# A row-sum kernel on one core: 120 consecutive rows per partition instead of 112, and 8 of the last 1,024 instead of 16

## The chip, the cores and the metric

The kernel runs on one core of a Trainium2 chip. Its time is the device time of one execution in microseconds (us); the median of several runs counts. Of the core's engines it uses VectorE (DVE in the profile), ScalarE (ACT) and SyncE (SP), which only issues transfers, and sixteen DMA engines that carry them.

## The reference

```python
batch, seq, dim = 32, 512, 1024
x = np.random.randn(batch, seq, dim).astype(np.float32)
multiplier = 0.5

def reference(x, multiplier):
    return (np.sum(x, axis=-1) * multiplier).astype(np.float32)
```

There are 32 x 512 = 16,384 rows of 1,024 numbers (4 KiB each, 64 MiB in all). Each row is summed and the sum halved; 64 KiB of results are written.

## The kernel before

The 16,384 rows are 128 per partition. They are cut in two regions. In the first, `x_rows` (line 43), each partition owns `own` = 112 consecutive rows; in the second, `x_last` (line 44), it owns 16 of the last 2,048. The results follow the same cut, `out_rows` and `out_last`, so that each partition's results are one run of bytes in each.

Rows are read in blocks of `B` = 16 per partition, 64 KiB per partition and 8 MiB in all, into three buffers `xb0` to `xb2`. All loads are issued by SP, so they share one DMA queue and stand in it in the order of issue. `load` (line 73) makes a load wait until the reduction that last read its buffer is done (`dve_done`), and gives each load a semaphore of its own. The first three loads wait for nothing; `start_loads_at_entry` puts them ahead of the kernel's start-up barrier.

Blocks 0 to 6 are the first region. For each, DVE waits for the load, sums the 16 rows in one `reduce_sum` (line 117) and multiplies the sums by 0.5 into `res` (line 123). In block 6 the last 8 rows go to ACT, one row per instruction (`act_row`, line 81, whose `accum_out` gives the scaled sum).

Block 7 is the second region. It is loaded in pieces of falling size, rows 0 to 7, 8 to 12, 13 to 14, and the last row in two parts of 544 and 480 numbers, so that little work is left when the last bytes land. Each piece's rows are split between ACT (`on_act`) and DVE (`dve_sum`, line 90, which adds the two halves of a row in one pass); the last row's two parts go to DVE.

There are two stores, both on SP. The early store (line 150) writes `res[:, 0:own]`; it waits for block 6 on DVE and on ACT and is issued once SP has issued all loads. The last store (line 175) writes `res[:, own:]` after the last row. SP then waits for both to land.

Of the kernel before, what the change touches and what calls it, by code (L numbers as in the profile page):

```python
# [9 lines left out]
def kernel(  # L10
# [13 lines left out]
    nc = tc.nc  # L24
# [10 lines left out]
    rows = N // P  # L35
    out_flat = out.rearrange("b s -> (b s)")
    mul = float(multiplier)

    B = 16
    n_blocks = rows // B  # L40
    assert N == P * rows and rows == n_blocks * B
    own = rows - B
    x_rows = x_flat[0 : P * own, :].rearrange("(p c) d -> p c d", p=P)
    x_last = x_flat[P * own : N, :].rearrange("(p c) d -> p c d", p=P)
    out_rows = out_flat[0 : P * own].rearrange("(p c) -> p c", p=P)
# [2 lines left out]
    def sbuf(name, *shape):  # L48
        return ctx.enter_context(nc.sbuf_tensor(name, list(shape), fp32)).ap()
# [4 lines left out]
    res = sbuf("res", P, rows)  # L54
    cut = 544
    at = 576
    end = sbuf("end", P, at + D - cut)

    def sem(name):
        return nc.alloc_semaphore(name=name)  # L60
# [5 lines left out]
    def marks(i, engine):  # L66

        s = dve_done if engine == "dve" else act_done
        i.then_inc(s, 1)
        counts[engine] += 1  # L70
        return counts[engine]

    def load(name, dst, src, free=None):
        landed = sem(name)
        i = nc.sync.dma_start(out=dst, in_=src)  # L75
        if free is not None:
            i.wait_op(dve_done, free, "sem-ge")
        i.then_inc(landed, 16)
        return landed

    def act_row(t, r, col):
        return nc.scalar.activation(  # L82
            out=t[:, r, :],
            in_=t[:, r, :],
            func=mybir.ActivationFunctionType.Copy,
            scale=mul,
            accum_out=res[:, col : col + 1],
        )

    def dve_sum(row, dst, scale):  # L90
        mid = row.shape[-1] // 2
        return nc.vector.tensor_tensor_reduce(  # L92
            out=row[:, 0:mid],
            in0=row[:, 0:mid],
            in1=row[:, mid:],
            scale=scale,
            scalar=0.0,
            op0=ADD,
            op1=ADD,
            accum_out=dst,  # L100
        )
# [3 lines left out]
    for b in range(n_blocks - 1):  # L105
        c0 = b * B
        t = buf[b % bufs]
        landed = load(
            f"landed{b}",
            t,  # L110
            x_rows[:, c0 : c0 + B, :],
            freed[b - bufs] if b >= bufs else None,
        )
        h = B if b < n_blocks - 2 else B // 2
        nc.vector.wait_ge(landed, 16)
        done = marks(
            nc.vector.reduce_sum(  # L117
                out=sums[:, c0 : c0 + h], in_=t[:, 0:h, :], axis=mybir.AxisListType.X
            ),
            "dve",  # L120
        )
        freed.append(done)
        scaled = nc.vector.tensor_single_scalar(  # L123
            out=res[:, c0 : c0 + h],
            in_=sums[:, c0 : c0 + h],
            scalar=mul,
            op=mybir.AluOpType.mult,
        )
        scaled.wait_op(dve_done, done, "sem-ge")
        early_dve = marks(scaled, "dve")  # L130
        if h < B:
            nc.scalar.wait_ge(landed, 16)
            for r in range(h, B):
                i = act_row(t, r, c0 + r)
            early_act = marks(i, "act")

    c0 = (n_blocks - 1) * B
    t = buf[(n_blocks - 1) % bufs]
    nc.sync.wait_ge(dve_done, freed[n_blocks - 1 - bufs])
    pieces = [(0, 8), (8, 13), (13, 15)]  # L140
    landed = [
        load(f"landed_p{k}", t[:, lo:hi, :], x_last[:, lo:hi, :])
        for k, (lo, hi) in enumerate(pieces)
    ]
    landed_end = [
        load(f"landed_e{k}", end[:, to : to + hi - lo], x_last[:, B - 1, lo:hi])
        for k, (to, lo, hi) in enumerate(((0, 0, cut), (at, cut, D)))
    ]
    nc.sync.wait_ge(dve_done, early_dve)
    early = nc.sync.dma_start(out=out_rows, in_=res[:, 0:own])  # L150
    early.wait_op(act_done, early_act, "sem-ge")
    early_stored = sem("early_stored")
    early.then_inc(early_stored, 16)

    on_act = {4, 5, 6, 7, 11, 12, 14}
    for k, (lo, hi) in enumerate(pieces):
        on = [r for r in range(lo, hi) if r in on_act]
        nc.scalar.wait_ge(landed[k], 16)
        for r in on:
            i = act_row(t, r, c0 + r)  # L160
        late_act = marks(i, "act") if k == len(pieces) - 1 else None
        on = [r for r in range(lo, hi) if r not in on_act]
        nc.vector.wait_ge(landed[k], 16)
        for r in on:
            dve_sum(t[:, r, :], res[:, c0 + r : c0 + r + 1], mul)
    nc.vector.wait_ge(landed_end[0], 16)
    first = dve_sum(end[:, 0:cut], end[:, at - 1 : at], 1.0)
    part = marks(first, "dve")
# [75 lines left out]
```

## Time and profile before

| What | Value |
|---|---|
| median of 3 runs | 160.72 us (160.71 to 160.73) |
| profiled execution | 160.73 us, span 159.4 us |
| DVE, ACT busy | 119.3 us (75%), 17.3 us (11%) |
| DMA packets, bytes | 2,016, 67.18 MB |
| early store | 56 KB, 10.8 us from issue to landing |
| last store | 8 KB, 1.4 us from issue to landing |

The profile is one execution; the span is the time between its first and last recorded event, and the time of the execution includes 1.3 us around it. In the timeline an instruction's row ends with the idle time of its engine before it and what ended it, in square brackets; "L117" is line 117 of the kernel. "SPq" is SP issuing a transfer, which is not the transfer itself. A packet is the part of a transfer that belongs to one partition here: 128 per load or store, eight for each DMA engine.

### The profile page before, as it was taken

The numbers are of one execution on the slowest core, as the hardware profiler recorded it, in microseconds if no ns is written. First come the engines' busy times: TensorE is split into PE (matmuls) and PEld (weight loads), VectorE is DVE, ScalarE is ACT, GpSimd is POOL, SyncE is SP. The second block draws the span as 40 slices with busy tenths as digits, with TensorE's granted clock in tenths as the row PEclk, the third lists the DMA queues.
The fourth block names the chain that finished last, engine by engine and source line by source line (L and its number), as shares of the span: only waits on it lengthen the run. The fifth ranks groups of instructions, "written<-read, shape, count | busy, mean of one in ns | idle before, by whom it ended". The sixth has DMA issues, their size and how long they took to land.

```text
span 159.4 us, 123 instructions
## 1 busy us (share of the span) xinstructions
DVE 119.3 (75%) x35; ACT 17.3 (11%) x31; POOL 0.2 (0%) x4
## 2 busy tenths in 40 slices
DVE  0000059998699968999599995999959999598644
ACT  3000000000000000000000000000000000397954
POOL 0000000000000000000000000000000000000000
DMA  7996996996998979969969969969979899698994
GB/s 263 526 526 263 526 526 263 526 510 280 526 428 362 526 345 444 526 280 510 526 263 526 526 263 526 510 280 526 477 312 526 378 411 526 288 493 359 437 402 143
DMA packets 2016, 67.18 MB, mean 421 GB/s; under 512 B 480, under 2 KB 608, under 8 KB 736
## 3 DMA queue, kind: packets, MB, share of 16 engines
q1 hardware_dynamic: 2016, 67.18, 98.0%
HBM read 67.11 MB, written 0.07 MB: 421 GB/s over the span
## 4 chain that ended last, share of the span: by engine, by line
DMA 76%; DVE 22%; SPq 1%; issue 0%
DMA xb<-in_x_dram 51%; DMA end<-in_x_dram 25%; DVE sums L117 22%; SPq L75 1%; DVE end L92 0%; DVE res L123 0%; DVE res L92 0%
## 5 line engine op out<-in xcount | busy, mean ns | idle before, releaser
L117 DVE TENSOR_REDUCE sums<-xb 128x16 f32<-128x16384 f32 (+1 forms) x7 | 112.0, 16001 | 30.8 <-DMA xb<-in_x_dram 30.8
L82 ACT ACTIVATE xb<-xb 128x1024 f32<-128x1024 f32 x15 | 15.7, 1045 | 137.7 <-DMA xb<-in_x_dram 137.7
L92 DVE CUSTOM_DVE_ANT_0 xb<-xb 128x512 f32<-128x512 f32 x8 | 5.1, 688 | 5.0 <-DMA xb<-in_x_dram 5.0
L82 ACT ACTIVATION_READ_ACCUMULATOR xb<-xb 128x1 f32 x15 | 2.8, 187 | 0.0
L103 DVE MEMSET end<- 128x2 f32 x1 | 0.1, 60 | 2.5 <-PEq L26 2.5
L82 ACT ACT_TABLE_LOAD x1 | 1.3, 1283 | 2.4 <-PEq L26 2.4
L123 DVE TENSOR_SCALAR res<-sums 128x16 f32<-128x16 f32 (+1 forms) x7 | 1.2, 174 | 0.2
L92 DVE CUSTOM_DVE_ANT_0 end<-end 128x272 f32<-128x272 f32 (+1 forms) x2 | 0.9, 426 | 0.2 <-DMA end<-in_x_dram 0.2
L92 DVE DVE_READ_ACCUMULATOR2_ANT res<- 128x1 f32 x9 | 0.7, 82 | 0.0
L225 POOL MEMSET const-bfloat16-1.0<- 128x1 bf16 x1 | 0.1, 101 | 0.0
L225 POOL MEMSET const-uint8-127<- 128x1 uint8 x1 | 0.1, 101 | 0.0
L225 POOL MEMSET const-float32-0.0<- 128x1 f32 x1 | 0.1, 98 | 0.2 <-issue 0.2
L225 POOL MEMSET const-float32-1.0<- 128x1 f32 x1 | 0.1, 98 | 0.0
L92 DVE DVE_READ_ACCUMULATOR2_ANT end<- 128x1 f32 x1 | 0.1, 83 | 0.0
## 6 DMA issues: line engine op xcount, KB each, us to landing
xb<-in_x_dram SPq DMA_DIRECT2D x1, 4096.0 KB, 31.1
xb<-in_x_dram SPq DMA_DIRECT2D x1, 2560.0 KB, 36.9
xb<-in_x_dram SPq DMA_DIRECT2D x1, 1024.0 KB, 38.9
end<-in_x_dram SPq DMA_DIRECT2D x1, 272.0 KB, 39.1
end<-in_x_dram SPq DMA_DIRECT2D x1, 240.0 KB, 39.2
xb<-in_x_dram SPq DMA_DIRECT2D x7, 40.8
out_dram<-res SPq DMA_DIRECT2D x1, 56.0 KB, 10.8
out_dram<-res SPq DMA_DIRECT2D x1, 8.0 KB, 1.4
```

Source lines behind the costliest of these rows:

```text
L75: i = nc.sync.dma_start(out=dst, in_=src)
L82: return nc.scalar.activation(out=t[:, r, :], in_=t[:, r, :], func=mybir.ActivationFunctionType.Copy, scale=mul, accum_out=res[:, col : co ...
L92: return nc.vector.tensor_tensor_reduce(out=row[:, 0:mid], in0=row[:, 0:mid], in1=row[:, mid:], scale=scale, scalar=0.0, op0=ADD, op1=ADD, ...
L103: marks(nc.vector.memset(end[:, at - 2 : at], 0.0), "dve")
L117: nc.vector.reduce_sum(out=sums[:, c0 : c0 + h], in_=t[:, 0:h, :], axis=mybir.AxisListType.X),
L123: scaled = nc.vector.tensor_single_scalar(out=res[:, c0 : c0 + h], in_=sums[:, c0 : c0 + h], scalar=mul, op=mybir.AluOpType.mult,)
L225: nc = _bacc.Bacc("TRN2", target_bir_lowering=False, num_devices=1)
```

## The change

`own` becomes 120: each partition owns 120 consecutive rows (480 KiB) in the first region and 8 of the last 1,024 (32 KiB) in the second. The loads keep their sizes and their order. The first piece of the last block (8 rows per partition) is now rows 112 to 119 of the first region; the pieces of 5 and 2 rows and the last row come from the second. The early store writes 120 results per partition (480 bytes, formerly 448) and waits for the first piece on DVE and ACT instead of for block 6; the last store writes 8 (32 bytes, formerly 64). The loop over the pieces therefore stands ahead of the early store in the text.

```diff
-    own = rows - B
+    tail = B // 2
+    own = rows - tail
 ...
-        early_dve = marks(scaled, "dve")
         if h < B:
             nc.scalar.wait_ge(landed, 16)
             for r in range(h, B):
-                i = act_row(t, r, c0 + r)
-            early_act = marks(i, "act")
+                act_row(t, r, c0 + r)
 ...
     pieces = [(0, 8), (8, 13), (13, 15)]
+    sources = [x_rows[:, c0:own, :], x_last[:, 0:5, :], x_last[:, 5:7, :]]
     landed = [
-        load(f"landed_p{k}", t[:, lo:hi, :], x_last[:, lo:hi, :])
-        for k, (lo, hi) in enumerate(pieces)
+        load(f"landed_p{k}", t[:, lo:hi, :], src)
+        for k, ((lo, hi), src) in enumerate(zip(pieces, sources))
     ]
     landed_end = [
-        load(f"landed_e{k}", end[:, to : to + hi - lo], x_last[:, B - 1, lo:hi])
+        load(f"landed_e{k}", end[:, to : to + hi - lo], x_last[:, tail - 1, lo:hi])
         for k, (to, lo, hi) in enumerate(((0, 0, cut), (at, cut, D)))
     ]
+
+    on_act = {4, 5, 6, 7, 11, 12, 14}
+    for k, (lo, hi) in enumerate(pieces):
+        nc.scalar.wait_ge(landed[k], 16)
+        nc.vector.wait_ge(landed[k], 16)
+        for r in range(lo, hi):
+            if r in on_act:
+                last_act = act_row(t, r, c0 + r)
+            else:
+                last_dve = dve_sum(t[:, r, :], res[:, c0 + r : c0 + r + 1], mul)
+        if k == 0:
+            early_act = marks(last_act, "act")
+            early_dve = marks(last_dve, "dve")
+    late_act = marks(last_act, "act")
     nc.sync.wait_ge(dve_done, early_dve)
     early = nc.sync.dma_start(out=out_rows, in_=res[:, 0:own])
     early.wait_op(act_done, early_act, "sem-ge")
 ...
-    on_act = {4, 5, 6, 7, 11, 12, 14}
-    for k, (lo, hi) in enumerate(pieces):
-        ...
```

More of the change, by code (lines that the diff above doesn't have):

```diff
@@ L153 @@
     early.then_inc(early_stored, 16)
-    on_act = {4, 5, 6, 7, 11, 12, 14}
-    for k, (lo, hi) in enumerate(pieces):
[L157 to L165, printed above, removed]
     nc.vector.wait_ge(landed_end[0], 16)
```

## The prediction

> **What bounds the kernel now.** I read the page first: its head, the engine shares, the slices and the DMA lines.
>
> ```profile
> span 159.4 us, 123 instructions
> ...
> DVE 119.3 (75%) x35; ACT 17.3 (11%) x31; POOL 0.2 (0%) x4
> ...
> DMA  7996996996998979969969969969979899698994
> ...
> q1 hardware_dynamic: 2016, 67.18, 98.0%
> HBM read 67.11 MB, written 0.07 MB: 421 GB/s over the span
> ...
> DMA 76%; DVE 22%; SPq 1%; issue 0%
> ```
>
> VectorE (DVE) is busy for 75% of the span, the DMA packets fill 98.0% of what sixteen DMA engines could do in it, and there is one queue, q1. So the transfers are the bound. The 22% that the chain gives to DVE says otherwise at first sight, so I read the chain of waits in order of time, and then the DVE rows of the timeline (start, duration, then what ended the idle time before).
>
> ```profile
> 0.43 40.72 DMA xb<-in_x_dram
> ...
> 118.30 39.18 DMA end<-in_x_dram
> 157.48 0.03 issue
> 157.51 0.41 DVE end L92
> ```
>
> ```profile
> 99.23 17.22 DVE L117 TENSOR_REDUCE sums<-xb 128x16 f32<-128x16384 f32 x1 [1.92 <-DMA xb<-in_x_dram]
> ...
> 118.57 17.22 DVE L117 TENSOR_REDUCE sums<-xb 128x16 f32<-128x16384 f32 x1 [1.91 <-DMA xb<-in_x_dram]
> ...
> 137.93 8.69 DVE L117 TENSOR_REDUCE sums<-xb 128x8 f32<-128x8192 f32 x1 [1.93 <-DMA xb<-in_x_dram]
> ...
> 146.91 0.35 SPq L150 DMA_DIRECT2D out_dram<-res  x1
> ...
> 147.64 0.69 DVE L92 CUSTOM_DVE_ANT_0 xb<-xb 128x512 f32<-128x512 f32 x1 [0.82 <-DMA xb<-in_x_dram]
> ...
> 151.72 0.19 ACT L82 ACTIVATION_READ_ACCUMULATOR xb<-xb 128x1 f32 x1
> 153.74 1.06 ACT L82 ACTIVATE xb<-xb 128x1024 f32<-128x1024 f32 x1 [1.84 <-DMA xb<-in_x_dram]
> ...
> 157.96 0.34 SPq L175 DMA_DIRECT2D out_dram<-res  x1
> ```
>
> Before every reduction DVE idles for about 1.9 us until a load lands, so each of these starts marks a landing: 118.57 - 99.23 = 19.34 and 137.93 - 118.57 = 19.36 us for 8 MiB, or 433 GB/s, with no hole between loads. A DVE link of 17.23 us in the chain only says which reduction freed a buffer; the load that it released then waited its turn (40.7 us to landing, two loads' worth). The span is therefore start (first reduction at 21.84, 2.5 us above one load of 19.35), then loads end to end until the last landing at 157.5, then a tail of 0.4 us on DVE and one small store (157.96 to 159.37, its 1.4 us to landing). The profiled execution took 160.73 us, 1.3 us around its span of 159.4; the median of the runs is 160.72, so the sum can be made against either.
>
> **The change, part by part.** The order of instructions on each engine is unchanged by the edit: DVE, ScalarE (ACT) and SP run the same instructions in the same order, seven loads of 64 KiB per partition, then 32, 20, 8, 2.1 and 1.9 KiB, then two stores. Four things differ.
>
> *1. The addresses of the loads.* Partitions now start 480 KiB apart in x instead of 448; the piece of 32 KiB per partition moves from the last region (64 KiB apart) to the main one (480); the pieces behind it are 32 KiB apart instead of 64. No row shows 480 or 32, so I bound by those that are there. At 448 KiB, 8 MiB take 19.36 us (433 GB/s). At 64 KiB, piece 0 takes 147.64 - 137.93 = 9.71 us for 4 MiB (432 GB/s), piece 1 153.74 - 147.64 = 6.10 us for 2.5 MiB (430). The trace's records of single packets, one per partition and load, explain the small fall by packet size alone: median 2,418 ns for 65,536 bytes, 1,213 for 32,768, 762 for 20,480, 311 for 8,192, 88 for 2,176, 25 for 448. All lie within 2 ns of 8 ns + bytes / 27.2 per ns. Eight packets per engine make the intervals: 8 x 2.418 = 19.34, 8 x 1.213 = 9.70, 8 x 0.762 = 6.10. A sevenfold change of the distance, odd multiple or power of two, thus left no mark on a packet. I take 0. The bounds: if the 56 large packets of an engine (56 x 2.418 = 135.4 us) ran at piece 1's rate instead of their own (433.4 / 429.7, 0.9%), the cost would be +1.2 us; in the other direction nothing below 8 ns + bytes / 27.2 is seen, except at the start, which is the second rival.
>
> A rule that speaks against such a change: the Trainium skill, "DMA: Bandwidth & Descriptors", section "Latency and other measured facts", lists copies between HBM tensors whose rows lie a large power of two apart as slow, 207 GB/s at 512 KiB and 103 at 4 MiB where 214 is full, and says that 4 KiB of padding restores it. By it 512 KiB would cost an estimated 3%, near 4.6 us here, while 480 KiB, which is 32 KiB off, would cost nothing; 32 KiB is a power of two, but below anything in its list. No run here shows 512 KiB.
>
> *2. The early store waits for more.* Before, SP waits for the last scaling by 0.5 (146.65 + 0.17) and issues 56 KB at 146.91. Now it waits for piece 0: DVE's fourth row ends near 150.2, ACT's row 7 at 151.72 + 0.19 = 151.91, so the issue moves to about 151.95, 5.0 us later. Behind it on SP there is only the wait for ACT's last row and the last store, which goes out at 157.96; all loads were issued by 118.8. On the ring the store stands behind the loads in either kernel: its packets first run at 156.5 and it lands at 146.91 + 10.8 = 157.7, just after the last load (157.48). From issue to first packet the last store needs 158.80 - 157.96 = 0.84 us, so the early one is ready near 152.8, 3.7 us ahead of its turn. Cost 0. Without that cover (issue after 155.7) it would slide later one for one, and would still have until 159.37 before it ended last.
>
> *3. The sizes of the stores.* Early: 480 bytes per partition instead of 448, by the line above 25.7 ns instead of 24.5; eight per engine, +0.01 us, ended long before 158.8. Last: 32 bytes instead of 64, 9.2 instead of 10.4 ns, 8 x 1.2 = -0.01 us on the path. What a 32-byte write costs in its confirmation no row shows. The time from the last packet's end to the last count of its semaphore is 0.38 us for the 64-byte store, 0.43 for the 1,920-byte load, 0.52 for the 448-byte store. So between -0.05 (a little less to confirm) and +0.14 (the dearest of those rows); I take the nearest row, the 64-byte one, hence 0.
>
> *4. The marks.* Two semaphore increments move from block 6's last instructions to piece 0's last; as many increments and waits as before, none on the path. 0.
>
> Sum: 160.73 + 0 + 0 - 0.01 + 0 = 160.72 against the profiled execution, 160.71 against the median. What is late stays late: the last load at 157.5.
>
> **The rivals.** *Slower: 480 KiB makes the DMA engines collide in the memory.* Place: the 56 large packets of each engine. Sixteen engines read in near lockstep (a load's sixteen completions lie within 0.5 us), each four partitions from its neighbour, formerly 1,792 and now 1,920 KiB. For it: the very first sixteen packets, which do start together, are the one group that is slow, 3.01 us in the mean against 2.42. Against it: all the later packets, at two distances, without a mark, and 1,920 = 15 x 128 is less even than 1,792 = 7 x 256. Price: at piece 1's rate +1.2 us, 161.9; if each of the seven loads lost the 0.59 us of the first wave, +4.1, 164.8. It decides from 0.32 us / 56 = 6 ns per packet, a median of 2,424. I take 161.9 as its time.
>
> *Faster: the first wave was a collision, and the new distance ends it.* The last engine to start (1.83 us) needed 2.74 us for its first packet, 0.32 above the rest, and the mean excess is 0.59; as the engines never idle afterwards, such a gain would reach the end: 160.1 to 160.4, say 160.3. Against it: the sixteen starts spread over 1.01 to 1.83, yet the first packets end between 4.02 and 4.57 almost regardless of their start (start 1.01 ends 4.29, start 1.52 ends 4.02), which looks like a common delay before the first data and not like addresses.
>
> *The stores decide.* A dear 32-byte confirmation, or one that comes early: +0.14 or -0.05 as above, which stays within 0.2%. To leave it, it would have to add another 0.2 us.
>
> **How the numbers follow.** 0.2% is 0.32 us, about what a measurement of this kernel can tell from no change. No change 0.68, at 160.6 to 160.9 (the bounds of the last store). Collisions 0.17. Faster first wave 0.09. The last store beyond its rows 0.06, 0.04 of it slower and 0.02 faster. So faster 0.09 + 0.02 = 0.11, same 0.68, slower 0.17 + 0.04 = 0.21. The range goes down to the faster rival's 160.3 and up to the slower one's 161.9, which leaves out about half of that rival and the lower part of the other, some 0.12.
>
> **What would show it.** Right: reductions still 19.35 us apart, large packets at 2,418 ns, early store issued near 152 with about 5.8 us to landing, last store 1.4 us. Collisions: intervals above 19.4 and a median above 2,424. The start: the first reduction before 21.5. The stores: a last landing other than 1.4 us after its issue. I am wrong if the time leaves 160.4 to 161.0 while the intervals between landings stay as they are.

## The result and the profile after

The changed kernel takes 160.94 us (median of 21 runs, 160.85 to 161.24), the kernel before 160.75 in the same comparison (21 runs, 160.62 to 161.12): a ratio of 1.0013, with a 95% interval of 1.0007 to 1.0018. It is slower by 0.2 us. The profiled executions say the same, 160.93 against 160.73.

The page of the changed kernel has the totals of before (the head, the engines, the queue, and the two stores with KB and us from issue to landing).

```profile
span 159.6 us, 123 instructions
...
DVE 119.3 (75%) x35; ACT 17.3 (11%) x31; POOL 0.2 (0%) x4
...
q1 hardware_dynamic: 2016, 67.18, 98.0%
...
out_dram<-res SPq DMA_DIRECT2D x1, 60.0 KB, 5.8
out_dram<-res SPq DMA_DIRECT2D x1, 4.0 KB, 1.4
```

The timeline of the changed kernel (start, duration, engine, line, operation, then the idle time before and what ended it), at the rows that the prediction used:

```profile
22.05 17.22 DVE L118 TENSOR_REDUCE sums<-xb 128x16 f32<-128x16384 f32 x1 [19.53 <-DMA xb<-in_x_dram]
41.38 17.22 DVE L118 TENSOR_REDUCE sums<-xb 128x16 f32<-128x16384 f32 x1 [1.90 <-DMA xb<-in_x_dram]
...
99.43 17.22 DVE L118 TENSOR_REDUCE sums<-xb 128x16 f32<-128x16384 f32 x1 [1.93 <-DMA xb<-in_x_dram]
...
118.78 17.22 DVE L118 TENSOR_REDUCE sums<-xb 128x16 f32<-128x16384 f32 x1 [1.92 <-DMA xb<-in_x_dram]
...
138.13 8.69 DVE L118 TENSOR_REDUCE sums<-xb 128x8 f32<-128x8192 f32 x1 [1.92 <-DMA xb<-in_x_dram]
...
147.84 0.69 DVE L93 CUSTOM_DVE_ANT_0 xb<-xb 128x512 f32<-128x512 f32 x1 [0.82 <-DMA xb<-in_x_dram]
...
152.13 0.35 SPq L164 DMA_DIRECT2D out_dram<-res  x1
...
158.16 0.34 SPq L178 DMA_DIRECT2D out_dram<-res  x1
```

And the first reduction of the kernel before, in its timeline:

```profile
21.84 17.22 DVE L117 TENSOR_REDUCE sums<-xb 128x16 f32<-128x16384 f32 x1 [19.31 <-DMA xb<-in_x_dram]
```

The last 139 us are the old ones, shifted: every row shown starts 0.20 or 0.21 us later (22.05 against 21.84, 138.13 against 137.93, 158.16 against 157.96), but for the early store, which has moved as foreseen. From the start of the first reduction to the end of the execution it is 160.93 - 22.05 = 138.88 us, and 160.73 - 21.84 = 138.89 before. All of the 0.2 us lie in front of the first reduction, in the landing of load 0.

The packet records show where. Each of the sixteen DMA engines carries eight packets of load 0, one after the other. (The records name no engine, but in both kernels every later packet of the seven large loads starts within 0.02 us of the end of an earlier one, so they fall into sixteen chains.) In the kernel before, the sixteen first packets take 3.02 us in the mean and the last of them ends 4.57 us into the span; now they take 3.23 us and the last ends at 4.78. The seven behind it take 2.42 us each in the mean in both kernels, so the first reduction starts 17.27 us after that last end in both (21.84 - 4.57, 22.05 - 4.78). Since no engine rests in these loads, whoever is late after its first packet is still late behind them.

### The profile page after: what moved, and what is told of

It reads as the page before. It is cut to its first block, busy times and chain, and to the rows that moved or that the text cites. A ratio compares the mean times of both kernels' runs of the same rounds, so it can differ in the third digit from the quotient of the medians.

```text
span 159.6 us, 123 instructions
## 1 busy us (share of the span) xinstructions
DVE 119.3 (75%) x35; ACT 17.3 (11%) x31; POOL 0.2 (0%) x4
## 4 chain that ended last, share of the span: by engine, by line
DMA 76%; DVE 22%; SPq 1%; issue 0%
DMA xb<-in_x_dram 51%; DMA end<-in_x_dram 25%; DVE sums L118 22%; SPq L76 1%; DVE end L93 0%; DVE res L93 0%
```

## Experiments

Theory 1: the places that load 0's first packets read set how far the last engine lags. Rivals: the stores; all loads at the new distance; a start that differs between any two programs. Each comparison has its own runs of the kernel before, whose medians lay between 160.73 and 160.82 us; the ratio follows the means of the runs, so that it can differ from the quotient of two medians where the runs scatter (452 KiB: 160.68 to 161.14). "Distance" is from the start of one partition's rows to the start of the next one's. The kernels that read rows of load 0, or of all loads, from elsewhere sum those other rows and serve only to measure time; "block 3 first" and the kernels with a head return the reference's results. "Last first packet" is the end, in us from the span's start, of the latest of the sixteen first packets of load 0, from the packet records; "rest" is the profiled execution less the start of its first reduction.

| Kernel | load 0's distance | last first packet | first reduction | rest | median | ratio (95%) |
|---|---|---|---|---|---|---|
| before | 448 KiB | 4.57 | 21.84 | 138.89 | 160.75 | 1 |
| changed | 480 | 4.78 | 22.05 | 138.88 | 160.94 | 1.0013 (1.0007 to 1.0018) |
| new stores, old reads | 448 | 4.60 | 21.89 | 138.89 | 160.79 | 1.0000 (0.9992 to 1.0009) |
| old, load 0 at 480 | 480 | 4.69 | 21.95 | 138.96 | 160.97 | 1.0013 (1.0004 to 1.0022) |
| new, load 0 at 448 | 448 | 4.59 | 21.86 | 138.92 | 160.78 | 1.0000 (0.9991 to 1.0009) |
| old, load 0 at 512 | 512 | 5.19 | 22.48 | 138.92 | 161.39 | 1.0039 (1.0027 to 1.0052) |
| old, load 0 at 64 | 64 | 4.67 | 21.92 | 138.94 | 160.86 | 1.0007 (0.9998 to 1.0016) |
| old, load 0 at 452 | 452 | 4.80 | 22.09 | 139.05 | 160.98 | 1.0006 (0.9997 to 1.0015) |
| old, load 0 at 416 | 416 | 5.33 | 22.60 | 138.93 | 161.46 | 1.0033 (1.0020 to 1.0046) |
| old, load 0 at 4 | 4 | 3.95 | 21.62 | 138.97 | 160.54 | 0.9984 (0.9975 to 0.9993) |
| old, block 3 first | 448 | 4.64 | 21.92 | 138.98 | 160.90 | 1.0009 (1.0000 to 1.0018) |
| new, block 3 first | 480 | 4.60 | 21.89 | 138.89 | 160.80 | 0.9999 (0.9991 to 1.0008) |
| old, all of x_rows at 512 | 512 | 5.08 | 22.38 | 139.09 | 161.47 | 1.0038 (1.0026 to 1.0050) |
| changed, once more | 480 | 4.67 | 21.97 | 138.92 | 160.97 | 1.0015 (1.0006 to 1.0024) |

**The change taken apart.** The first run puts all reads of the changed kernel back:

```diff
-    x_rows = x_flat[0 : P * own, :].rearrange("(p c) d -> p c d", p=P)
-    x_last = x_flat[P * own : N, :].rearrange("(p c) d -> p c d", p=P)
+    x_rows = x_flat[0 : P * (rows - B), :].rearrange("(p c) d -> p c d", p=P)
+    x_last = x_flat[P * (rows - B) : N, :].rearrange("(p c) d -> p c d", p=P)
...
-    sources = [x_rows[:, c0:own, :], x_last[:, 0:5, :], x_last[:, 5:7, :]]
+    sources = [x_last[:, lo:hi, :] for lo, hi in pieces]
...
-        load(f"landed_e{k}", end[:, to : to + hi - lo], x_last[:, tail - 1, lo:hi])
+        load(f"landed_e{k}", end[:, to : to + hi - lo], x_last[:, B - 1, lo:hi])
```

> The changed kernel with the addresses of all its loads put back to those before (448 KiB apart, the last block from the last 2,048 rows), so it stores sums of other rows in places; stores, their sizes and the early store's later issue stay as changed. Theory 1 (the 0.2 us come from the addresses of the first load, whose first sixteen packets end later): about 160.75 us, first reduction starts near 21.84. Rival (the stores, or the early store's later issue): about 160.94 and the first reduction near 21.84. Rival (something about the start that differs between any two programs): first reduction anywhere from 21.7 to 22.1, and the time with it.

The second and third exchange load 0 alone:

```diff
+    x_first = x_flat[0 : P * 120, :].rearrange("(p c) d -> p c d", p=P)   # P * 112 in the changed kernel
...
-            x_rows[:, c0 : c0 + B, :],
+            (x_first if b == 0 else x_rows)[:, c0 : c0 + B, :],
```

> The kernel before with one edit: block 0 is read with partitions 480 KiB apart instead of 448 (so block 0's sums are of other rows). Theory 1: about 160.94, first reduction near 22.05, all later reductions 19.35 apart. Rival (every load at 480 loses a little): about 160.77, 0.03 of the 0.2. Rival (stores): 160.75.

> The changed kernel with one edit: block 0 is read with partitions 448 KiB apart (its sums are of other rows); loads 1 to 7 and the stores stay as changed. Theory 1: about 160.75, first reduction near 21.84. Rivals (all loads, or the stores): about 160.92.

The first reduction in the timelines of these three, in this order:

```profile
21.89 17.22 DVE L118 TENSOR_REDUCE sums<-xb 128x16 f32<-128x16384 f32 x1 [19.38 <-DMA xb<-in_x_dram]
```

```profile
21.95 17.22 DVE L118 TENSOR_REDUCE sums<-xb 128x16 f32<-128x16384 f32 x1 [19.43 <-DMA xb<-in_x_dram]
```

```profile
21.86 17.22 DVE L119 TENSOR_REDUCE sums<-xb 128x16 f32<-128x16384 f32 x1 [19.34 <-DMA xb<-in_x_dram]
```

Load 0 at 480 KiB brings the whole 0.13% into the old kernel (160.97); load 0 at 448 takes all of it out of the changed one (160.78), whose other loads and stores stay changed; and the new stores with the old reads show no cost (1.0000). Theory 1 stands and the three rivals fall: no part of the stores or of loads 1 to 7 is seen, and the intervals leave them at most 0.09%. A start that differs between any two programs falls too: three programs with the old places of load 0 start at 21.84, 21.89 and 21.86 us, two with the new ones at 22.05 and 21.95. In the second run's profile the start moved by 0.11 instead of 0.21 us; one profile is one draw (the changed kernel once more gave 21.97), and the medians carry the size.

> The changed kernel once more, for the spread of its first wave: first reduction 21.95 to 22.1, 160.95 us, 0.13% above the kernel before. If it lies at 21.85 in this profile while the median stays at 160.95, one profile is not enough to rank two addresses.

It measured 160.97 us, 1.0015, so the effect repeats.

**Is there a rule in the distance?** The same edit with other values of rows per partition in `x_first`: 128, 16, 113 and 104, and, as the last, a pattern that lets partition p start at row p.

> The kernel before with block 0 read with partitions 512 KiB apart (other rows). Theory 1 in the form that engines collide when their addresses differ by a large power of two: the first packets last longer than the 3.0 and 3.2 us means seen, the first reduction starts after 22.05, by 0.2 to some us. Theory 1 without that form (any address has its own start): between 21.7 and 22.2. No effect of addresses: 21.84 and 160.75.

> The kernel before with block 0 read with partitions 64 KiB apart, one run of 8 MiB (other rows). Theory A (the first packets of the sixteen engines collide when the addresses four partitions apart, here 256 KiB, share a large power of two; 448 gives 7 x 256 KiB): a start as with 448, first reduction 21.85 to 21.9, 160.8 us. Theory B (the first touch of far-apart places costs; 64 KiB keeps the whole load in 8 MiB instead of some 56): a start better than with 448, first reduction 21.2 to 21.6, 160.2 to 160.5.

> The kernel before with block 0 read with partitions 452 KiB apart (113 rows; four partitions are 113 x 16 KiB apart). Theory A: fewer collisions than any distance before, first reduction 21.3 to 21.7, 160.2 to 160.6 us. Theory B: as with 448, 21.85 and 160.8.

> The kernel before with block 0 read with partitions 416 KiB apart (104 rows; four partitions are 13 x 128 KiB apart, as 480 gives 15 x 128). Theory A: as with 480, first reduction 21.95 to 22.05, 161.0 us. Theory B: as with 448, 21.85 and 160.8.

> The kernel before with block 0 read with partitions 4 KiB apart (partition p reads rows p to p + 15, so rows are read up to sixteen times and the whole load touches 0.6 MB). Theory A: a spread of small distances, no collisions, first reduction 21.2 to 21.6. Theory B: also an early start, by the same amount or more. Neither: 21.85 or later; then the delay of the first packets belongs to the start of the queue and not to where they read.

The first reductions at 512, 416 and 4 KiB, from their timelines:

```profile
22.48 17.22 DVE L118 TENSOR_REDUCE sums<-xb 128x16 f32<-128x16384 f32 x1 [19.97 <-DMA xb<-in_x_dram]
```

```profile
22.60 17.22 DVE L118 TENSOR_REDUCE sums<-xb 128x16 f32<-128x16384 f32 x1 [20.08 <-DMA xb<-in_x_dram]
```

```profile
21.62 17.22 DVE L118 TENSOR_REDUCE sums<-xb 128x16 f32<-128x16384 f32 x1 [19.09 <-DMA xb<-in_x_dram]
```

The start alone is worth anything from 21.62 to 22.60 us, and the rest stays at 138.9 to 139.1. The rest is highest, by up to 0.2 us, in two profiles (452 KiB, and all of `x_rows` at 512 below): there the piece of 2.5 MiB landed 6.26 and 6.33 us after the piece before it instead of 6.10, although its addresses were the old ones. Both theories of a rule fall. Theory A (collisions by powers of two) expected 452 KiB, four partitions 113 x 16 KiB apart, to be the best; it was no better than 448. It expected 416 to be like 480, and 416 is the worst of all. Theory B (far-apart places are dear) expected 64 KiB, one run of 8 MiB, to gain 0.3 to 0.6 us; it gained nothing. Only the load that touches 0.6 MB in all is early, its first packets at 2.63 us in the mean and the last end at 3.95; of the 0.62 us gained there, 0.4 are lost again in its later packets, which read rows that the neighbours read too: every second wave of sixteen has a mean of 2.45 to 2.47 us instead of 2.42, and the first reduction gains only 0.22 us (21.62 against 21.84).

A last end is a start and a length, and the places move both. The first packet that ends last starts at 1.83 us and takes 2.74 in the kernel before, 1.24 and 3.54 in the changed one, 1.19 and 4.15 at 416 KiB, but 2.10 and 3.09 at 512. At 512 KiB the first packets are shorter in the mean (3.09 us) than at 480 (3.23); the lag there is a late start.

**Differences or places?** One edit in both kernels; the work is the same and complete:

```diff
-        c0 = b * B
+        c0 = [3, 0, 1, 2, 4, 5, 6][b] * B
```

> The kernel before, with blocks loaded and summed in the order 3, 0, 1, 2, 4, 5, 6 (results are the reference's): load 0 keeps its distance of 448 KiB, and each engine starts 192 KiB further on. Theory C (only the differences between the engines' addresses matter): first reduction 21.85, 160.8 us. Theory D (the places themselves matter, each set has its own start): first reduction anywhere from 21.6 to 22.6, off 21.85 by over 0.1, and the time 138.9 us above it.

> The changed kernel with the same order 3, 0, 1, 2, 4, 5, 6 (results are the reference's): load 0 at 480 KiB, each engine 192 KiB further on. Theory C: as the changed kernel, 21.95 to 22.05 and 160.95 us. Theory D: off that by over 0.1; if it starts before 21.85 the changed layout is as good as the old one, and before 21.6 better.

The first reductions of these two:

```profile
21.92 17.22 DVE L117 TENSOR_REDUCE sums<-xb 128x16 f32<-128x16384 f32 x1 [19.39 <-DMA xb<-in_x_dram]
```

```profile
21.89 17.22 DVE L118 TENSOR_REDUCE sums<-xb 128x16 f32<-128x16384 f32 x1 [19.38 <-DMA xb<-in_x_dram]
```

The differences between the engines' places stay, and all places move by 192 KiB. The changed kernel loses its 0.2 us by it: all eleven runs lie in 160.72 to 160.89, against 160.85 to 161.24 for the changed kernel as it is. The old one goes the other way, by 0.08 us, at the edge of its interval. Neither first reduction moved by the 0.1 us asked for beyond doubt (21.89 against 21.97 and 22.05; 21.92 against 21.84), so the profiles alone would not decide; the medians speak for theory D, places and not only differences.

**The later loads.** With `x_first = x_flat[0 : P * 128, :]` for every block of the first region:

> The kernel before with blocks 0 to 6 read with partitions 512 KiB apart (the sums of blocks 0 to 6 are of other rows); block 7 as it was. First-wave theory: as with block 0 alone at 512, first reduction near 22.48, reductions 19.35 apart, 161.4 us. Rival (every load loses at a power of two): reductions over 19.4 apart; by 3% they would be 19.9 apart and the time 165 to 166 us.

The first three reductions in its timeline:

```profile
22.38 17.22 DVE L118 TENSOR_REDUCE sums<-xb 128x16 f32<-128x16384 f32 x1 [19.86 <-DMA xb<-in_x_dram]
...
41.71 17.22 DVE L118 TENSOR_REDUCE sums<-xb 128x16 f32<-128x16384 f32 x1 [1.90 <-DMA xb<-in_x_dram]
...
61.05 17.22 DVE L118 TENSOR_REDUCE sums<-xb 128x16 f32<-128x16384 f32 x1 [1.92 <-DMA xb<-in_x_dram]
```

The spacing is 19.33 and 19.34 us, and the time that of load 0 alone at 512 (161.47 against 161.39). The Trainium skill ("DMA: Bandwidth & Descriptors", "Latency and other measured facts") has copies between HBM tensors at 512 KiB 3% below full rate (207 of 214 GB/s). These loads into SBUF lose nothing by the distance after the first packets, and the measurement decides for them.

**Short first packets.** Load 0 is cut in two transfers, a head of some bytes of each partition and the rest, both waited for by the first reduction:

```diff
+        if b == 0:
+            head = load("landed_head", t[:, 0:1, :], x_rows[:, 0:1, :])
+        lo = 1 if b == 0 else 0
...
-            t,
-            x_rows[:, c0 : c0 + B, :],
+            t[:, lo:, :],
+            x_rows[:, c0 + lo : c0 + B, :],
...
+        if b == 0:
+            nc.vector.wait_ge(head, 16)
```

> The kernel before with load 0 cut in two transfers, the first row of each partition (4 KiB packets) and the other fifteen. Eight packets more per engine cost about 8 x 8 ns = 0.06 us. If engines that are late stay late whatever the packet size: first reduction 21.85 to 22.0, 160.8 to 161.0 us. If short first packets let the engines settle cheaply: first reduction below 21.6, about 160.5 us.

> The changed kernel with load 0 cut as in the run of the old one (first row of each partition in a transfer of its own; results are the reference's). If the engines' lags arise while long first packets run, the old and the new distance now start alike: first reduction 21.6 to 21.75, 160.6 us, the 0.2 us gone. If they come from what the places cost whatever the packet: 0.2 us above the old kernel with the same cut, 21.9 and 160.8.

> The changed kernel with a shorter first transfer, 1 KiB of each partition (results are the reference's). Short packets settle the engines: 21.5 to 21.7, 160.5 to 160.6 us. Lag belongs to the places: 21.9 and 160.8. The long packets only meet the same trouble a little later: 22.0 and 160.95.

> The kernel before with the first 1 KiB of each partition in a transfer of its own (results are the reference's). Short packets settle the engines: 21.5 to 21.7, 160.5 to 160.6 us, as the changed kernel with the same cut. Otherwise 21.85 to 21.9, 160.8.

> The kernel before with the first two rows of each partition (8 KiB) in a transfer of their own (results are the reference's): 128 packets that last 8 x 0.31 = 2.5 us in all at full speed, against 1.3 us for one row and 0.35 us for 1 KiB. If the slow stretch at the start lies at a fixed time and is cheaper for short packets: as good as one row or better, 160.4 to 160.6 us. If one row was luck: 160.8.

> The kernel before with the first row of each partition in a transfer of its own, once more: 160.55 to 160.7 us and a ratio of about 0.999, if its 160.63 was no accident; 160.8 if it was.

| Kernel, head per partition | first reduction | median | ratio (95%) |
|---|---|---|---|
| old, 4 KiB | 21.69 | 160.63 | 0.9995 (0.9986 to 1.0003) |
| old, 4 KiB, again | 21.66 | 160.67 | 0.9995 (0.9987 to 1.0004) |
| new, 4 KiB | 22.00 | 160.88 | 1.0004 (0.9995 to 1.0013) |
| old, 8 KiB | 21.71 | 160.56 | 0.9991 (0.9982 to 1.0000) |
| old, 1 KiB | 22.58 | 161.37 | 1.0030 (1.0019 to 1.0041) |
| new, 1 KiB | 22.50 | 161.26 | 1.0031 (1.0019 to 1.0042) |

The first reduction of the old kernel with a head of 4 KiB, and of 1 KiB:

```profile
21.69 17.22 DVE L122 TENSOR_REDUCE sums<-xb 128x16 f32<-128x16384 f32 x1 [18.70 <-DMA xb<-in_x_dram]
```

```profile
22.58 17.22 DVE L124 TENSOR_REDUCE sums<-xb 128x16 f32<-128x16384 f32 x1 [19.59 <-DMA xb<-in_x_dram]
```

With a 1 KiB head the head's packets are all done by 1.78 us, and then the sixteen first long ones take 3.05 us (old) and 3.17 us (new) in the mean instead of the 2.38 to 2.40 of the waves behind them: the slow stretch is not used up by 128 short packets, it is met later. The old kernel loses 0.5 us by it. The new one is 0.5 us above the kernel before, but only 0.3 above itself without a head (161.26 against 160.97 in the same comparison). With 4 KiB, the sixteen first packets take 0.39 us (old) and 0.59 us (new) in the mean instead of 0.16, and the long ones behind them are at full speed. So the long packets that start between 1.5 and 2.4 us, behind 1 KiB, are slow, and those that start from 2.6 us (old) or 2.9 us (new) on, behind 4 KiB, are not (in the three profiles one of 48 took 2.41 us, the others 2.27). Whether the stretch ends after a time or after an amount read, these runs do not separate; it is not one time for all places, since at 64 KiB three of the first packets start at 1.95 to 2.19 us and take 2.42 to 2.43. The new distance still starts later than the old with the same cut (22.00 against 21.69); the intervals of the two ratios overlap, so this difference is likely and not proven. A head of 8 KiB in the old kernel is the fastest version with the reference's results, 160.56 us against 160.73 in its comparison, but its interval reaches 1.0000: I do not call it faster.

## Why the prediction was wrong

The size was inside the range and within the 0.2% that I had called the limit of a measurement; but 21 runs of each tell some 0.06% apart, and the sign is clear, where I had forecast a hair faster. That 160.94 lies inside the range is luck: the part above 160.9 was there for packets that are slow throughout, and these did not occur.

- **The step that failed** is part 1, the addresses of the loads, "I take 0". For the 55 of an engine's 56 large packets that follow its first, it holds: spacing 19.33 to 19.36 us in the changed kernel, 2.42 us per packet. For the sixteen first packets it does not: their last end moved from 4.57 to 4.78 us, which is the whole result. The 0 rested on median packets, and a median of 896 says nothing of the first sixteen.
- **The rival that named the place had one sign only.** The prediction saw that the first wave was slow and that the end would inherit what the last engine lost there, but priced only that the new distance might end the lag (-0.32 to -0.59 us). The same rows allow more lag as well as less, and the bound of the part should have been two-sided: the other starts tried here reach -0.22 to +0.76 us (21.62 and 22.60 against 21.84).
- **What was read wrongly.** That first packets ended between 4.02 and 4.57 whatever their start "looks like a common delay" was taken as evidence against addresses. Other addresses move the last end anywhere between 3.95 and 5.33, so addresses are in it. Two figures that the prediction took from the packet records are a little off, without weight in the sum: the first sixteen take 3.02 us in the mean, not 3.01, and the median 8,192-byte packet 309 ns, not 311.
- **The slower rival** (large packets slowed throughout) did not occur: the median packet stays at 2,418 ns, at 512 KiB too.
- **The stores** went as worked out: the early one issued at 152.13 (predicted 151.95, plus the shift of 0.2), 5.8 us to landing, and the last one 1.4 us, with 32-byte writes as with 64. The run with the new stores and the old reads puts their joint effect at 1.0000 (0.9992 to 1.0009).

That the places of load 0 cause the 0.2 us is shown, by the exchange in both directions. What stays open is what in the memory or on the way to it makes one set of places slower at the start than another. The runs exclude the two rules tried and put the cause into the sixteen first packets; no record here shows which engine reads which place, or what it waits for.

## What to carry to other kernels

Where the DMA engines never rest, as here, the end was set by the engine that lagged most after its first packet, and nothing behind it made up for that: when a change moves addresses, bound the first load's start on both sides, separately from the rate. To find such an effect, subtract the first landing from the whole time; if the rest is the same (138.88 and 138.89 us here), everything behind the first landing is cleared at once. Do it in more than one profile: over all runs the rest varied by 0.2 us, as much as the effect. Which addresses start well has to be measured, with enough runs that 0.1% can be seen.

## What the hardware showed that I had not expected

- A load of 8 MiB, first in the queue, lands between 21.6 and 22.6 us depending on where it reads, and not in the order of the distances: 4 KiB is the earliest (21.62), 512 and 416 are the latest (22.48, 22.60). The four between, 448, 64, 480 and 452 (21.84 to 22.09), are too close for one profile each to rank: the changed kernel itself gave 22.05 and 21.97.
- A load that stands at the head of the queue as 1 KiB packets makes the next, large packets slow (3.05 to 3.17 us instead of 2.38), while 4 or 8 KiB packets take the slow stretch on themselves and leave the next ones at full speed.
- From then on the median time of a packet is 8 ns and its bytes at 27.2 per ns, within 6 ns for every size in the two kernels, at distances of 32, 64, 448 and 480 KiB, and also for the 64 KiB packets at 512.
